# Output projection of feed-forward 1: gated tiles loaded through ScalarE's queue, ten weight tiles kept for the second pass, two rows of modulation computed in the mixer

## The chip, the core and the metric

The kernel runs on one core of a Trainium2 chip. The core has a matrix engine (TensorE, PE in the profile, with its weight loads as PEld), VectorE (DVE), ScalarE (ACT), GpSimd (POOL), SyncE (SP), which here only issues transfers, and 16 DMA engines that move data between device memory and the on-chip memory. Each engine executes its own instructions strictly in order. An instruction that waits holds back all that stand behind it on its engine; a transfer is started by an instruction too, here nearly always one of SyncE.

The metric is the time of one execution on the device in microseconds (us), median of three runs.

## The reference

One layer of a diffusion backbone works on 512 latent tokens and 256 context tokens of width 1024. Three sub-layers follow each other: a SwiGLU feed-forward of inner width 2816, a mixer (four heads of a chunkwise mLSTM and four groups of a pooling mixer), and a second feed-forward. Each is wrapped in RMS norms whose shift, scale and gate come from a modulation vector of nine rows of 1024 that is computed from the conditioning:

```
def ada_in(x, mod, j, g):
    return rmsnorm(x, g) * (1 + mod[:, 3 * j + 1, None]) + mod[:, 3 * j, None]

def ada_out(x, z, mod, j, g, res_w):
    return x + res_w * mod[:, 3 * j + 2, None] * rmsnorm(z, g)

def swiglu(y, w_in, w_out):
    a, b = jnp.split(y @ w_in, 2, axis=-1)
    return (jax.nn.silu(a) * b) @ w_out
...
        mod = (sc @ w_mod[l] + b_mod[l]).reshape(-1, N_MOD, D_MODEL)
        x = ada_out(x, swiglu(ada_in(x, mod, 0, norm_pre[l, 0]), ffn_w_in[l, 0], ffn_w_out[l, 0]),
                    mod, 0, norm_post[l, 0], 0.5)
        p = ada_in(x, mod, 1, norm_pre[l, 1]) @ w_in[l]
```

Rows 0 to 2 of the modulation belong to feed-forward 1, rows 3 to 5 to the mixer, rows 6 to 8 to feed-forward 2. The context tokens have a modulation of their own, which is needed up to row 4.

## The kernel before

All values are 32 bit. A product is formed as three matmuls of two halves: each operand is split into a high part (a rounding cast, ScalarE, line 81) and a low part (the difference, VectorE, line 78), and high times high, low times high and high times low are summed (`mm3`, lines 96 to 99, and `mm3p`, lines 107 to 110, through `mm` at line 102, whose order is fixed).

**Feed-forward 1** works on 768 tokens. For each of 22 inner tiles of 128 (f = 0 to 21) it computes the gated tile `silu(a) * b` (`in_fast`) and stores it to device memory (`g_d[f]`, line 492). The output projection then has two passes, `out_pass(0, ...)` and `out_pass(1, ...)`, each for 384 tokens (three token tiles) and all 22 inner tiles. They are called pass 1 and pass 2 in what follows. `prepare(f)` loads the tile of the output weight (line 756) and the gated tile (line 759) and splits both; `product` does the matmuls, 18 for each f, which accumulate in six banks of PSUM (`pa` and `pz`). The last two inner tiles of pass 1, and the last four of pass 2, are multiplied token tile by token tile, so that each token tile's sum is complete early. `done1`, through `ada_tile`, then normalises it: two squares of the sum (ScalarE, line 148), an inverse root on GpSimd (lines 159 and 143), gain and residual on VectorE (lines 175 and 179), the square of the result z (ScalarE, line 148 again), a second inverse root and the scaling (line 187). `back` transposes the result (TensorE, line 105), applies shift and scale (ScalarE, line 199) and splits it into `yh` and `yl` (lines 203 and 204), the operands of the mixer. `Backs` lets these transposes happen a number of steps (its lag) after their token tile. Pass 2 begins with the four inner tiles whose split weights are still in place, and then goes backward through the others. Latent token tiles also store z to device memory (`x1_d`, line 185).

**The modulation rows** 2 to 8 are computed beside this by `mod_steps`, a generator. A row (a block in the code) takes eight loads of a 128x1024 weight tile (line 676), each followed by one VectorE instruction for each stream that adds weight times conditioning to an accumulator (line 678; rows 2 to 4 have two streams, latent and context), and a last step: a sum over partitions on TensorE (line 688), the norm's gain (loaded in pieces, line 697; multiplied at line 698), and small stores of the row (line 704). `filler(n)` takes n steps; `mod_tick` takes one at most places of feed-forward 1, `out_pass` one or two after each inner tile. When row 4 is done, `begin_chain` loads and transposes what the passes' ends need.

**The mixer** begins with the value projection (lines 868 to 870 copy its results), whose gate columns go through a row of dependent instructions on VectorE and ScalarE (lines 880 to 935: logarithm of the forget gates, four scans along the tokens, exponentials). TensorE needs their results for transposes (`rows_to_columns`); until then it has projections as fillers. `MIX` lists the order of its steps by hand and how many microseconds of fillers stand between them.

Engines execute in the order that a scheduler has written: it may move an instruction ahead of others, except those that are pinned (`pin`, `keep_in_program_order`) relative to each other. Buffers come from pools: `m4` has 6 buffers, `raw` 5, `q3` 10.

## Time and profile before

| | |
|---|---|
| median of 3 runs | 1171.31 us (1171.27 to 1172.27) |
| the profiled execution | 1170.85 us, span of the trace 1169.1 us |
| granted TensorE clock, mean | 0.983 |
| TensorE busy | 1111.0 us (95% of the span) |
| VectorE busy | 894.8 us (77%) |
| ScalarE busy | 530.6 us (45%) |
| GpSimd busy | 106.4 us (9%) |
| DMA | 169.25 MB, mean 145 GB/s |
| feed-forward 1, inner products | to 372.4 us |
| output projection, pass 1 | 373.6 to 474.3 us |
| output projection, pass 2 | 485.6 to 590.1 us |

The span goes from the first to the last instruction; an execution has some 1.75 us around it. An engine's busy time doesn't say whether it bounds a stage: TensorE at 95% leaves 58 us in all, and where these lie is read from slices, from the timeline and from what ended each idle stretch.

### The profile page before, as it was taken

The numbers are of one execution on the slowest core, as the hardware profiler recorded it, in microseconds if no ns is written. First come the engines' busy times: TensorE is split into PE (matmuls) and PEld (weight loads), VectorE is DVE, ScalarE is ACT, GpSimd is POOL, SyncE is SP. The second block draws the span as 40 slices with busy tenths as digits, with TensorE's granted clock in tenths as the row PEclk, the third lists the DMA queues.
The fourth block names the chain that finished last, engine by engine and source line by source line (L and its number), as shares of the span: only waits on it lengthen the run. The fifth ranks groups of instructions, "written<-read, shape, count | busy, mean of one in ns | idle before, by whom it ended". The sixth has DMA issues, their size and how long they took to land.

```text
span 1169.1 us, 17262 instructions
## 1 busy us (share of the span) xinstructions
PE 1111.0 (95%) x6610; PEld 1004.8 (86%) x6610; DVE 894.8 (77%) x1315; ACT 530.6 (45%) x910; POOL 106.4 (9%) x139
## 2 busy tenths in 40 slices
PE   4999999999999999599899799999999999999996
PEld 3899999999998877478699687888999899999995
DVE  3798997898798676557445867875899898888865
ACT  4544333333333333464364556557665344444431
POOL 4000000000000000200122314412000000000001
PEclk9999999999999999799999899999999999999999
DMA  9933433643544887549623112134334333333321
GB/s 306 287 121 104 151 124 100 200 133 97 184 153 127 328 301 274 190 159 324 215 83 99 37 63 64 64 109 148 123 91 120 116 108 109 109 108 109 107 75 73
DMA packets 152673, 169.25 MB, mean 145 GB/s; under 512 B 7415, under 2 KB 125687, under 8 KB 152589
## 3 DMA queue, kind: packets, MB, share of 16 engines
q1 hardware_dynamic: 152540, 168.12, 44.6%
q8 instruction: 52, 0.85, 0.3%
q14 instruction: 33, 0.26, 0.1%
q10 hardware_dynamic: 48, 0.01, 0.0%
HBM read 153.12 MB, written 14.98 MB: 144 GB/s over the span
## 4 chain that ended last, share of the span: by engine, by line
PE 47%; DVE 6%; ACT 2%; DMA 1%; issue 1%; POOL 1%; SPq 0%; DVEq 0%; ACTq 0%; POOLq 0%
PE pa L102 9%; PE pa L98 7%; PE pa L99 7%; PE pa L97 7%; PE pz L102 4%; PE pz L97 3%; PE pz L98 3%; PE pz L99 3%; PE pt L102 3%; PE pt L105 1%; DVE wins L78 1%; DMA raw<-in_w_in_dram 1%; ACT junk L148 1%; DMA q<-g 0%; DVE z L179 0%
## 5 line engine op out<-in xcount | busy, mean ns | idle before, releaser
L97 PE MATMUL pa<-yh,wins 128*128 128x256 f32 (+1 forms) x768 | 236.2, 308 | 0.7 <-ACT yh L81 0.4
L99 PE MATMUL pa<-yl,wins 128*128 128x256 f32 (+1 forms) x768 | 235.9, 307 | 0.0
L98 PE MATMUL pa<-yh,wins 128*128 128x256 f32 (+1 forms) x768 | 235.8, 307 | 0.0
L78 DVE TENSOR_TENSOR wins<-raw,wins 128x1024 fp32r<-128x1024 f32 (+1 forms) x144 | 156.6, 1087 | 70.5 <-PE pa L98 39.8
L81 ACT CAST wins<-raw 128x1024 fp32r<-128x1024 f32 (+1 forms) x146 | 136.2, 935 | 110.5 <-PE pa L99 36.9
L97 PEld LDWEIGHTS pa<-yh,wins 128*128 128x128 f32 x768 | 145.0, 189 | 3.0 <-issue 0.8
L99 PEld LDWEIGHTS pa<-yl,wins 128*128 128x128 f32 x768 | 144.9, 189 | 0.5
L98 PEld LDWEIGHTS pa<-yh,wins 128*128 128x128 f32 x768 | 144.9, 189 | 0.5
L99 PE MATMUL pa<-tl,wins 128*128 128x384 f32 (+1 forms) x388 | 122.3, 315 | 0.0
L98 PE MATMUL pa<-th,wins 128*128 128x384 f32 (+1 forms) x388 | 121.8, 314 | 0.0
L97 PE MATMUL pa<-th,wins 128*128 128x384 f32 (+1 forms) x388 | 121.3, 313 | 0.0
L678 DVE SCALAR_TENSOR_TENSOR m<-m,sc,m 128x1024 f32<-128x1024 f32 x80 | 100.2, 1278 | 9.6 <-DMA m<-in_w_mod_dram 5.9
L81 ACT CAST wins<-sw 128x1024 fp32r<-128x1024 f32 x78 | 81.7, 1047 | 48.9 <-PE pa L99 35.5
L78 DVE TENSOR_TENSOR wins<-sw,wins 128x1024 fp32r<-128x1024 f32 x78 | 95.2, 1221 | 10.7 <-PE pa L98 7.0
L102 PE MATMUL pa<-yh,wins 128*128 128x512 f32 (+2 forms) x352 | 97.0, 362 | 0.0
L97 PEld LDWEIGHTS pa<-th,wins 128*128 128x128 f32 x388 | 72.8, 188 | 0.9 <-issue 0.8
L99 PEld LDWEIGHTS pa<-tl,wins 128*128 128x128 f32 x388 | 73.0, 188 | 0.1
L98 PEld LDWEIGHTS pa<-th,wins 128*128 128x128 f32 x388 | 73.0, 188 | 0.0
L102 PEld LDWEIGHTS pa<-yh,wins 128*128 128x128 f32 x352 | 62.0, 191 | 9.2 <-issue 2.2
L97 PE MATMUL pa<-wins,q 128*128 128x512 f32 x148 | 55.3, 407 | 8.9 <-ACT q L81 8.9
L102 PE MATMUL pa<-yl,wins 128*128 128x512 f32 (+2 forms) x176 | 62.4, 355 | 0.5 <-DVE yl L78 0.5
L98 PE MATMUL pa<-wins,q 128*128 128x512 f32 x148 | 59.3, 400 | 1.2 <-DVE q L78 1.2
(388 smaller groups left out, 2177.1 us busy)
## 6 DMA issues: line engine op xcount, KB each, us to landing
raw<-in_ffn_w_in_dram SPq DMA_DIRECT2D x87, 512.0 KB
raw<-in_ffn_w_out_dram SPq DMA_DIRECT2D x62, 512.0 KB
m<-in_w_mod_dram SPq DMA_DIRECT2D x57, 512.0 KB
g<-q SPq DMA_DIRECT2D x22, 384.0 KB
q<-g SPq DMA_DIRECT2D x44, 192.0 KB
raw<-in_w_in_dram SPq DMA_DIRECT2D x16, 512.0 KB
raw<-in_w_mod_dram SPq DMA_DIRECT2D x11, 512.0 KB
raw<-in_w_out_dram SPq DMA_DIRECT2D x16, 256.0 KB
```

The lines of the kernel that those rows point to most:

```text
L78: return eng.tensor_tensor(out=out_ap, in0=a, in1=b, op=ALU.subtract)
L81: return S.copy(hi, src)
L97: T.matmul(out_ap, lhsT=wh, rhs=xh, start=first, stop=False, **kw)
L98: T.matmul(out_ap, lhsT=wl, rhs=xh, start=False, stop=False, **kw)
L99: T.matmul(out_ap, lhsT=wh, rhs=xl, start=False, stop=last, **kw)
L102: return tc.keep_in_program_order(T.matmul(*args, **kw))
L105: return tc.keep_in_program_order(T.transpose(**kw))
L148: return S.activation(out=junk, in_=src, func=AF.Square, scale=D ** -0.5, accum_out=ssq)
L678: V.scalar_tensor_tensor(out=accs[st], in0=w, scalar=sc[:, st * KD + k:st * KD + k + 1], in1=accs[st], op0=ALU.mult, op1=ALU.add)
```

## The change

Five things are changed together. The gated tiles are loaded by ScalarE's queue instead of SyncE's, five inner tiles ahead (`fetch`, pinned), and so are the stores of z (`x1_d`), which moreover stand behind z's square now, and the small stores of the modulation rows. Ten weight tiles instead of four are kept split for pass 2; six of them lie in `yh` and `yl`, so the transposes that write these come 14 steps after their token tile instead of 4. Rows 7 and 8 of the modulation leave `out_pass`; they are computed in the mixer, a step at every fourth entry of `MIX` from the thirteenth on, with weights in `raw` and an accumulator of their own (`macc`). The norm's gain of a row is loaded ahead of its eight steps, where it isn't one of these two. `filler` is called at every tick of feed-forward 1 after the 17th, and in the passes once for every second inner tile.

```
@@ ada_tile
+        r2 = rstd1(z, junk)
         if store is not None:
-            load(store, z)
-        r2 = rstd1(z, junk)
+            put(store, z)
@@ done1
-                            lambda: q3()[:, 0:512], pin)
+                            lambda: q3()[:, 0:512], pin, nc.scalar.dma_start)
@@ mod_steps
-        def mod_steps():
-            for blk, streams in ((2, (0, 1)), (3, (0, 1)), (4, (0, 1)), (5, (0,)), (6, (0,)), (7, (0,)), (8, (0,))):
+        def mod_steps(blocks, new, acc, ahead):
+            for blk, streams in blocks:
...
+                res = gains() if ty and ahead else None
                 for k in range(KD):
-                    w = m4()
+                    w = new()
                     load(w, w_mod[k * P:(k + 1) * P, blk * D:(blk + 1) * D])
...
                 for st, i, g, cs in at:
-                    load(rows[(blk, st)][:, cs], res[g:g + 1])
+                    nc.scalar.dma_start(rows[(blk, st)][:, cs], res[g:g + 1])
                 yield blk
-        steps = mod_steps()
+        steps = mod_steps([(b, (0, 1)) for b in (2, 3, 4)] + [(b, (0,)) for b in (5, 6)], m4, m4, True)
@@ mod_tick
-            if next(count) % 4 < 3:
+            i = next(count)
+            if i % 4 < 3 or i > 16:
@@ out_pass
+            def fetch(f):
+                raws[f] = q3()[:, 0:384]
+                pin(nc.scalar.dma_start(raws[f], g_d[f][:, c0:c0 + 384]))
             def prepare(f):
...
-                r = q3()[:, 0:384]
-                load(r, g_d[f][:, c0:c0 + 384])
                 g = q3(F32R)
-                gs[f] = split_w(r, to=(g[:, 0:384], g[:, 384:NT]), keep=pin)
+                gs[f] = split_w(raws[f], to=(g[:, 0:384], g[:, 384:NT]), keep=pin)
...
+            for f in order[:5]:
+                fetch(f)
             for f in order[:2]:
                 prepare(f)
-            for f, later in zip(order[:-tail], order[2:]):
-                prepare(later)
+            for i, f in enumerate(order[:-tail]):
+                for g in order[i + 5:i + 6]:
+                    fetch(g)
+                prepare(order[i + 2])
...
-                filler(2 if half == 0 and f % 3 == 0 else 1)
+                if i % 2:
+                    filler(1)
@@ the passes
-        backs, first_backs = Backs(4), Backs(4)
+        backs, first_backs = Backs(4), Backs(14)
+        kept = order[-10:-4]
+        places = [y.rearrange("p k c -> p (k c)")[:, i * D:(i + 1) * D] for i in range(6) for y in (yh, yl)]
+        homes = {f: lambda i=i: (places[2 * i], places[2 * i + 1]) for i, f in enumerate(kept)}
...
-        for f in order[:-4]:
+        for f in order[:-10]:
             wos.pop(f)
-        order = order[-4:] + order[-5::-1]
+        order = order[-10:] + order[-11::-1]
@@ the mixer's loop
+        late = mod_steps([(7, (0,)), (8, (0,))], raw, lambda: pool.tile([P, D], F32, tag="macc", name="macc", bufs=1), False)
+        for i, step in enumerate(MIX.split()):
+            if i > 8 and i % 4 == 0:
+                next(late, None)
```

The scheduler's order moves at three places. The first is ScalarE at the border between the passes. Before, with the squares of the third token tile's sum (`pz`), the first transposes' results (L199, L203), the square of the third z (`thz`), and the first casts of pass 2:

```order
L148 ACTIVATE junk_116,sm_4307<-pz_3477 128x512
L148 ACTIVATE junk_116,sm_4307<-pz_3478 128x512
L199 ACTIVATE q3_4322<-pt_4323,ycol1_3623 128x128 x4
L203 CAST yh_103<-q3_4322 128x4x128
L148 ACTIVATE junk_116,sm_4344<-thz_3472 128x1024
L81 CAST q3_4360<-q3_4358 128x384
L81 CAST q3_4365<-q3_4363 128x384
```

The same place of the change:

```order
L148 ACTIVATE junk_116,sm_4247<-pz_3555 128x512
L148 ACTIVATE junk_116,sm_4247<-pz_3556 128x512
L148 ACTIVATE junk_116,sm_4271<-thz_3550 128x1024
L186 DMA x1_0_105<-thz_3550 128x1024
L763 DMA q3_4286<-g_12_129 128x384
L763 DMA q3_4288<-g_13_130 128x384
L763 DMA q3_4290<-g_14_131 128x384
L763 DMA q3_4292<-g_15_132 128x384
L763 DMA q3_4294<-g_16_133 128x384
L81 CAST q3_4296<-q3_4286 128x384
L81 CAST q3_4299<-q3_4288 128x384
```

The transposes' results are gone from here; a store and five loads stand between the last square and the first cast.

The second place is ScalarE at the start of pass 1, behind the last two activations of feed-forward 1 (L382, L385). Before:

```order
L382 ACTIVATE q3_3363<-pa_3367 128x384
L385 ACTIVATE q3_3363<-q3_3363 128x384
L81 CAST sw_3481<-raw_3479 128x1024
L81 CAST q3_3487<-q3_3485 128x384
L81 CAST wins_3492<-raw_3490 128x1024
```

The same place of the change:

```order
L382 ACTIVATE q3_3431<-pa_3435 128x384
L385 ACTIVATE q3_3431<-q3_3431 128x384
L763 DMA q3_3557<-g_0_117 128x384
L763 DMA q3_3559<-g_1_118 128x384
L763 DMA q3_3561<-g_2_119 128x384
L763 DMA q3_3563<-g_3_120 128x384
L763 DMA q3_3565<-g_4_121 128x384
L81 CAST sw_3569<-raw_3567 128x1024
L81 CAST q3_3573<-q3_3557 128x384
```

Five loads stand ahead of the first cast of pass 1. On VectorE two modulation steps (line 692 of the change) stand among the last four instructions of feed-forward 1, and four of row 6 stand directly ahead of the split of weight tile 18; all eight weight tiles of row 6 share one buffer of `m4`.

The third place is VectorE at the head of the mixer, from the copy of the forget gates (L881 before, L901 of the change) to the scans. Before:

```order
L881 COPY h4_5601<-h4_5600 64x768
L885 SCALAR_TENSOR_TENSOR h4_5602<-h4_5601 64x768
L893 MEMSET h4_5603 64x768
L896 MEMSET h4_5605 64x768
L894 MEMSET h4_5603 32x6
L895 MEMSET h4_5603 32x6
L888 SCALAR_TENSOR_TENSOR h4_5601<-h4_5601,h4_5602 64x768
L78 TENSOR_TENSOR wins_6031<-raw_6028,wins_6030 128x1024
L898 SCALAR_TENSOR_TENSOR h4_5604<-h4_5603,h4_5601 32x768
```

The same place of the change:

```order
L692 SCALAR_TENSOR_TENSOR macc_5855<-raw_5944,sc_99,macc_5855 128x1024
L901 COPY h4_5462<-h4_5461 64x768
L692 SCALAR_TENSOR_TENSOR macc_5855<-raw_5991,sc_99,macc_5855 128x1024
L905 SCALAR_TENSOR_TENSOR h4_5463<-h4_5462 64x768
L913 MEMSET h4_5464 64x768
L916 MEMSET h4_5466 64x768
L914 MEMSET h4_5464 32x6
L915 MEMSET h4_5464 32x6
L692 SCALAR_TENSOR_TENSOR macc_5855<-raw_6095,sc_99,macc_5855 128x1024
L692 SCALAR_TENSOR_TENSOR macc_5855<-raw_6133,sc_99,macc_5855 128x1024
L908 SCALAR_TENSOR_TENSOR h4_5462<-h4_5462,h4_5463 64x768
L78 TENSOR_TENSOR wins_5898<-raw_5895,wins_5897 128x1024
```

Four steps of row 7 stand in between here (L692). A fifth stands behind the second scan, and a sixth ahead of the first L1095 (L1075 before), which comes ahead of the copies of `tcol` (L959 before, L979 of the change).

## Rows read from the trace of the kernel before

**Rows 1.** Page, part 2: TensorE's busy tenths in 40 slices of 29.2 us.

```profile
PE   4999999999999999599899799999999999999996
```

**Rows 2.** Chain of waits, 355 to 700 us: start, us, what.

```profile
484.48 3.17 DMA q<-g
584.79 5.48 PE pz L102 x24
```

**Rows 3.** Timeline of TensorE, 455 to 500 us: start, us, instruction, count [idle before].

```profile
461.31 0.85 PE L102 MATMUL pa<-wins,q 128*128 128x512 f32 x3
465.18 6.30 PE L102 MATMUL pa<-wins,q 128*128 128x512 f32 x20 [0.81 <-DVE q L78]
471.31 2.94 PE L102 MATMUL pz<-wins,q 128*128 128x512 f32 x12
485.64 1.65 PE L97 MATMUL pa<-wins,q 128*128 128x512 f32 x3 [8.90 <-ACT q L81]
492.35 0.40 PE L97 MATMUL pz<-wins,q 128*128 128x512 f32 x1
```

**Rows 4.** Timelines of ScalarE and SyncE, 455 to 500 us.

```profile
484.04 1.06 ACT L148 ACTIVATE junk<-thz 128x1024 bf16<-128x1024 f32 x1 [0.90 <-DVE thz L179]
485.10 0.50 ACT L81 CAST q<-q 128x384 fp32r<-128x384 f32 x1
484.03 0.34 SPq L185 DMA_DIRECT2D x<-thz  x1
```

**Rows 5.** Windows: span, busy us of each engine, granted clock, DMA share, GB/s.

```profile
core 0: us, PE busy (x) PEld busy (x) DVE busy (x) ACT busy (x) POOL busy (x), PEclk, DMA share, GB/s
477.00:493.00 16.00, 6.16 (x15) 4.43 (x16) 10.64 (x15) 7.01 (x16) 3.87 (x7) 0.57 0.52 173
625.00:661.80 36.80, 28.66 (x166) 24.51 (x165) 32.56 (x51) 19.57 (x27) 15.31 (x11) 0.92 0.36 94
```

**Rows 6.** Timeline of TensorE, 555 to 600 us.

```profile
568.01 0.84 PE L102 MATMUL pa<-sw,q 128*128 128x512 f32 x3
573.03 0.49 PE L102 MATMUL pa<-wins,q 128*128 128x512 f32 x1 [2.83 <-ACT q L81]
590.11 0.60 PE L105 MATMUL pt<-ident,m 128*128 128x128 f32 x4
```

**Rows 7.** Timelines of ScalarE and SyncE, 540 to 600 us.

```profile
563.74 0.51 ACT L81 CAST q<-q 128x384 fp32r<-128x384 f32 x1 [9.25 <-DMA q<-g]
560.24 1.12 SPq L704 DMA_DIRECT2D row<-m  x4
561.41 0.34 SPq L759 DMA_DIRECT2D q<-g  x1
```

**Rows 8.** Timelines of VectorE and TensorE at the head of the mixer.

```profile
635.28 0.95 DVE L888 SCALAR_TENSOR_TENSOR h<-h,h 64x768 f32<-64x768 f32 x1 [1.43 <-ACT h L887]
658.29 2.08 DVE L1075 SCALAR_TENSOR_TENSOR h<-h,pcol,h 128x770 f32<-128x770 f32 x2 [0.53 <-ACT h L1072]
655.48 1.08 PE L105 MATMUL pt<-ident,h 128*128 128x128 f32 x6 [3.64 <-ACT h L927]
660.69 0.66 PE L105 MATMUL pt<-ident,h 64*128 64x64 f32 x4 [4.14 <-DVE tcol L959]
```

**Rows 9.** Instructions of line 678: min/median/max ns, first and last start.

```profile
L678 DVE SCALAR_TENSOR_TENSOR m<-m,sc,m x80: 1272/1278/1285, 112.8 to 541.6; 128x1024 f32<-128x1024 f32 x80
```

**Rows 10.** Timelines of TensorE, ScalarE and VectorE at pass 1's start.

```profile
372.39 1.06 PE L688 MATMUL pt<-m,ones 128*32 128x512 f32 x8
375.77 0.50 PE L98 MATMUL pa<-sw,q 128*128 128x512 f32 x1 [0.56 <-DVE q L78]
369.97 0.53 ACT L385 ACTIVATE q<-q 128x384 f32<-128x384 f32 x1 [3.31 <-DVE q L384]
372.49 0.56 DVE L392 TENSOR_TENSOR q<-q,pa 128x384 f32<-128x384 f32 x1 [0.89 <-PE pa L99]
374.03 1.22 DVE L78 TENSOR_TENSOR sw<-raw,sw 128x1024 fp32r<-128x1024 f32 x1
```

More of the change, by code (lines that the diff above doesn't have):

```diff
@@ L167, in tile_layer, with ada_tile @@
     x2_d = [dpool.tile([P, D], F32, name=f"x2_{t}") for t in range(4)]
-    def ada_tile(t, zs, z, halves, xr, gc, store, nxt, junk, half, keep=lambda ins: ins):
+    def ada_tile(t, zs, z, halves, xr, gc, store, nxt, junk, half, keep=lambda ins: ins, put=load):
         r = rstd2(halves)
@@ L664, in query_key, with gains @@
             S.mul(wqk, kc(p), float(P) ** -0.5)
-        def mod_steps():
-            for blk, streams in ((2, (0, 1)), (3, (0, 1)), (4, (0, 1)), (5, (0,)), (6, (0,)), (7, (0,)), (8, (0,))):
+        def mod_steps(blocks, new, acc, ahead):
+            for blk, streams in blocks:
                 accs = {}
+                j, ty = divmod(blk, 3)
+                nq = 4 // len(streams)
+                n = D // nq
+                at = [(st, i, 32 * (nq * st + i), slice(i * n, (i + 1) * n)) for st in streams for i in range(nq)]
+                def gains():
+                    gb = new()[:, 0:n]
+                    src = norm_pre if ty == 1 else norm_post
+                    for st, i, g, cs in at:
+                        load(gb[g:g + 32], src[j:j + 1, cs].broadcast_to([32, n]))
+                    return gb
                 for st in streams:
-                    accs[st] = m4()
+                    accs[st] = acc()
                     G.memset(accs[st], 0.0)
                     load(accs[st][0:1, :], b_mod[blk:blk + 1, :])
+                res = gains() if ty and ahead else None
                 for k in range(KD):
-                    w = m4()
+                    w = new()
                     load(w, w_mod[k * P:(k + 1) * P, blk * D:(blk + 1) * D])
@@ L681, in mod_steps @@
                 yield
-                nq = 4 // len(streams)
-                n = D // nq
-                at = [(st, i, 32 * (nq * st + i), slice(i * n, (i + 1) * n)) for st in streams for i in range(nq)]
                 p = pt()[:, 0:n]
@@ L688, in mod_steps @@
                     T.matmul(p[g:g + 32], lhsT=ones.broadcast_to([P, 32]), rhs=accs[st][:, cs], start=True, stop=True)
-                j, ty = divmod(blk, 3)
-                res = m4()[:, 0:n]
                 if ty == 0:
+                    res = new()[:, 0:n]
                     S.copy(res, p)
                 else:
-                    gb = m4()[:, 0:n]
-                    src = norm_pre if ty == 1 else norm_post
-                    for st, i, g, cs in at:
-                        load(gb[g:g + 32], src[j:j + 1, cs].broadcast_to([32, n]))
-                    V.scalar_tensor_tensor(out=res, in0=p, in1=gb, op1=ALU.mult,
+                    res = res if ahead else gains()
+                    V.scalar_tensor_tensor(out=res, in0=p, in1=res, op1=ALU.mult,
                                            **(dict(scalar=1.0, op0=ALU.add) if ty == 1 else
@@ L1255, in tile_layer @@
         queue = [sources[x[0]](*map(int, x[1:])) for x in QUEUE.split()]
-        for step in MIX.split():
+        late = mod_steps([(7, (0,)), (8, (0,))], raw, lambda: pool.tile([P, D], F32, tag="macc", name="macc", bufs=1), False)
+        for i, step in enumerate(MIX.split()):
+            if i > 8 and i % 4 == 0:
+                next(late, None)
             what, arg = step[0], step[1:]
@@ L1275, in tile_layer @@
                     {"w": hd.weights, "s": hd.states, "d": hd.decays, "o": hd.outputs}[what](int(arg[1]))
+        for _ in late:
+            pass
         junk = pool.tile([P, D], BF16, tag="un", name="junk2", bufs=2)
```

9 lines of the change are left out of this document (5 added, 4 removed).

## Prediction

> **What bounds the kernel now.** I read the page's slices first [rows 1]: TensorE is busy in nearly every slice, so the time can change only where its digit drops: slice 17 (467 to 497 us), slices 20 and 23, and what a change adds where it is full. Those places are the border between the two passes of the output projection, the end of the second pass, and the head of the mixer. The timeline of TensorE and what ended each idle stretch give each place; the chain of waits gives the price of a load and of a matmul at full speed: 24 matmuls in 5.48 us, 0.228 us each [rows 2].
>
> - End of pass 1: the last two tiles' 36 matmuls begin at 461.31 and end at 471.31 + 2.94 = 474.25 [rows 3]. At full speed they need 8.2 us, so 12.94 − 8.2 = 4.7 us is lost, of which 0.2 is the last matmul's tail: 4.5 us. They waited for the last tiles' splits.
> - Border: the second pass begins at 485.64, 11.4 us after the end; ScalarE casts its first gated tile only after the last token tile's square (484.04), which stands ahead of it on the same engine [rows 3, 4]. The load had landed. The next 12 matmuls take until 492.35, 6.71 us for 2.74 us of work: in this stretch the granted clock is 0.57, close to the lower level of 1.2 GHz, after TensorE stood idle [rows 3, 5].
> - End of pass 2: 72 matmuls from 568.01 to 590.11, 22.1 us for 16.4 [rows 6]: 5.7 us lost. ScalarE stood 9.25 us for a gated tile whose load SyncE issued only at 561.41, behind four small stores of a modulation row at 560.24 [rows 7].
> - Mixer: between 625 and 661.8 TensorE is busy 28.66 of 36.8 us, VectorE 32.56 [rows 5]; TensorE waits 3.64 us for ScalarE's L927 and 4.14 us for VectorE's L959 [rows 8], both ends of VectorE's row of scans.
>
> **The change, part by part.** I sum against the profiled execution, 1170.85 us (span 1169.1 and 1.75 around it); the median of the runs is 1171.31, 0.46 above, and the forecast is given on that.
>
> *End of pass 1: −4.5.* Of the 26 modulation loads in this pass 16 are left, and gated tiles are loaded five ahead, so the splits of tiles 18 to 21 should be done early. One thing is behind them: block 6 now has a single buffer for its weights, and four of its steps stand on VectorE directly ahead of tile 18's split. A step costs 1.28 us [rows 9] and its load about 3.2 [rows 2], so these four are a chain of some 18 us. Splits need only some 3 us a tile against 4.1 us (18 × 0.228) of matmuls, so by then they should be about four tiles (16 us) ahead, and two more tiles of matmuls lie between. I take the whole 4.5; the other end is 0.
>
> *Border: +2.6.* Before, the first gated tile lay ready. Now ScalarE's order is: third square, store of x1, five loads, then the cast. The three token tiles' chain stays as it was (square ends near 474.25 + 10.8; I give it 0.5 back, since VectorE's modulation steps beside it are gone), so 10.3. From a store's issue (484.03) to the landing of the gated tile issued behind it (484.48 + 3.17 = 487.65) took 3.6 us [rows 2, 4]; a cast takes 0.5 [rows 4]. TensorE starts at 10.3 + 3.6 + 0.5 = 14.4 us after the end instead of 11.4. Counting what is not work: before 11.4 − 0.45 (four transposes) + 3.97 (6.71 − 2.74) = 14.9; after 14.4 + about 3.1 (the same 6.4 us at half clock, without the wait for a low half in it) = 17.5. Ends: 0, if the loads are issued while ScalarE waits, which its order excludes, and +5. The kept weights save the loads and splits of six tiles here, but nothing waits for those loads.
>
> The Trainium skill ("DMA: Bandwidth & Descriptors", "Rules for kernel authors") advises to issue a transfer early and wait late, so that its fixed cost overlaps. Here it is issued late by its place on ScalarE; by that rule, with the load out before the squares, the border would cost 3.6 less. The trace agrees: before, the tile that was loaded early was cast without a wait for it, at 485.10.
>
> *Start of pass 1: +2.7.* The same on a smaller scale. ScalarE's last activation of feed-forward 1 ends at 369.97 + 0.53 = 370.5 [rows 10]; behind it now stand five loads. The first lands at 370.5 + 3.2, its cast ends at 374.2; TensorE, which did 1.16 us of row sums until 373.55 here and does these earlier now, is free at 372.39 [rows 10]. VectorE has two modulation steps among its last four instructions: the first takes the idle 0.89 before L392 and 0.4 more, the second 1.28, so the low half of the first weight tile moves from 374.03 to 375.6 and L98 from 375.77 to 377.3 [rows 10]. Loss then: 377.3 − 372.39 − 1.37 (six matmuls) = 3.5; before: 375.77 − 373.55 − 1.37 = 0.85. The difference is 2.7; ends 0 and 6.
>
> *End of pass 2: −5.7.* The gated tiles no longer stand behind SyncE's row stores, and ScalarE's order now has tiles 3 to 0 ahead of the casts of the mixer's value weights. Block 6's copy and four row stores stand ahead of tile 3 on ScalarE and wait for TensorE, but two tiles of matmuls (8.2 us) cover them, the copy and five issues of 0.34 [rows 7]; without this cover they would cost about 3. Ends −5.7 and 0.
>
> *Transposes* of the first half move from early to late in pass 2: same count, same cost. The six kept tiles' two splits each (1.2 us a tile on VectorE) were not waited for.
>
> *Head of the mixer: +7.4.* Block 7's steps are on VectorE in the row of scans. Two stand around L901, which waits for nothing else: +2.56 [rows 9]. Two stand between L905 and L908, where VectorE idled 1.43 us before [rows 8]: 2.56 − 1.43 = +1.1. One stands behind the first two scans: +1.28. That is +5.0 at TensorE's first wait (3.64). At the second (4.14), the copies that free its bank stood behind two L1075 of 1.04 us [rows 8]; now three or four and one more step stand ahead, of which 0.53 idle covers part: +2.4. Low end 0 (all hidden), high end 8 × 1.28 = 10.2. I take 7.4, since each inserted step stands between instructions that depend on each other.
>
> *Rest of the mixer: +1.5.* Eight steps of block 8, two times four row stores on ScalarE and two row sums. TensorE is full there and its fillers cover VectorE; ends 0 and 10.2, nearer to 0. The row sums that leave the passes (8 matmuls twice) come back here: 0.
>
> Sum: −4.5 + 2.6 + 2.7 − 5.7 + 7.4 + 1.5 = +4.0: 1174.85 by the profile, **1175.3** by the median. About 0.2% (2.3 us) is what a measurement tells from no change.
>
> **The rivals.**
> *Faster: the mixer hides block 7.* If VectorE's scans are not what TensorE waits for at 655 and 661, or the steps fall into its idle time, the 7.4 is gone: 1167.9. It decides from below 1.1 us in that place. For it: VectorE has 4.2 us idle between 625 and 661.8. Against it: only 2 of these lie where the steps are. Chance 0.2.
> *Half of it: no change.* Only the three steps that nothing can hide cost (3.8), and the rest falls together with ScalarE's table loads: 1171.7. Chance 0.12.
> *Slower: tile 18 late.* The single buffer's chain of 18 us is longer than the lead, TensorE waits for tile 18 and the 4.5 isn't won, or more is lost: 1180 to 1183. For it: splits were hardly a tile ahead before. Against it: ten of the 26 modulation loads that shared the pass with them are gone. Chance 0.15.
> *The gated loads were short of bandwidth, not of a queue.* Then ScalarE's queue brings nothing and the 5.7 stays: 1181. The trace: once issued, the load of 561.41 was there at 563.74, 2.3 us later [rows 7]. Chance 0.05. The Trainium skill speaks for this ("DMA: Bandwidth & Descriptors", "Issuing engines are not separate DMA queues"): transfers from any engine share the same 16 DMA engines, and another issuer saves only issuing time. The trace shows the issue itself held back by what is ahead on SyncE, which that rule leaves open.
>
> **How the numbers follow.** Forecast 0.48, rivals 0.2, 0.12, 0.15, 0.05. The forecast's own range is 1171 to 1180. With the rivals on both sides the range is 1166 to 1182. Faster 0.2; same 0.12 and 0.06 of the forecast's low side, 0.18; slower 0.62.
>
> **What would show it.** End of pass 1: no idle in the 36 matmuls. Border: TensorE idle 14 us, ScalarE's first cast waiting for the gated load, not for an engine. Start: L98 waiting some 2 us for VectorE. End of pass 2: 72 matmuls in 16.5 us. Mixer: the first wait of TensorE near 8.6 us, the second near 6.5, VectorE full from 630 on. The forecast is wrong if the mixer's waits stay near 3.6 and 4.1, if the border stays at 11, or if TensorE waits for tile 18.

## The result, and the profile after

The changed kernel takes 1189.87 us (median of 4 runs, 1188.3 to 1193.28) against 1171.3 us: ratio 1.016, interval 1.0136 to 1.0184, so 18.6 us slower. The forecast was 1175.3, slower, with a range up to 1182; the sign was right and the size was not. The profiled execution took 1188.92 us (span 1186.8). Of its page, the span, TensorE's slices (of 29.7 us each) and the granted clock, which answer to [rows 1]:

```profile
span 1186.8 us, 17172 instructions
...
PE   4999999999998999699997798899999999999996
...
PEclk9999999999999999799999799999999999999999
```

Counted from 1, slice 17 (475 to 504 us) is still the border. Slice 13 (356 to 386 us), where the first pass starts, has lost a tenth. In the mixer slices 22, 23, 25 and 26 stand below 9, where there was one. The timeline of TensorE of the changed kernel gives the places, in the columns of [rows 3]:

```profile
376.60 1.19 PE L97 MATMUL pa<-sw,q 128*128 128x512 f32 x4 [0.27 <-ACT q L81]
...
380.88 0.50 PE L98 MATMUL pa<-sw,q 128*128 128x512 f32 x1 [2.63 <-DVE q L78]
...
464.77 5.66 PE L102 MATMUL pa<-wins,q 128*128 128x512 f32 x24
470.27 2.90 PE L102 MATMUL pz<-wins,q 128*128 128x512 f32 x12
...
486.32 0.80 PE L97 MATMUL pa<-yh,q 128*128 128x512 f32 x1 [13.16 <-ACT q L81]
...
566.65 0.84 PE L102 MATMUL pa<-sw,q 128*128 128x512 f32 x3
...
583.08 0.60 PE L105 MATMUL pt<-ident,m 128*128 128x128 f32 x4
...
654.75 1.54 PE L105 MATMUL pt<-ident,h 128*128 128x128 f32 x6 [9.90 <-ACT h L947]
661.44 0.66 PE L105 MATMUL pt<-ident,h 64*128 64x64 f32 x4 [5.15 <-DVE tcol L979]
...
737.02 0.98 PE L698 MATMUL pt<-macc,ones 128*32 128x256 f32 x8 [2.37 <-issue]
...
761.62 1.51 PE L105 MATMUL pt<-ident,h 128*128 128x128 f32 x6 [2.67 <-DVE h L1215]
```

The 36 matmuls of the first pass's tail run through (464.77 to 473.17; before, waits of 1.69 and 0.81 us stood in them), and so do the 72 of the second pass's tail (566.65 to 583.08). The border waits 13.16 us. The second pass ends at 583.08, where it ended at 590.11 [rows 6]: the passes are 7.0 us ahead. In the mixer the first wait is 9.90 us instead of 3.64 and the second 5.15 instead of 4.14 [rows 8]. Then there are places that the prediction did not name: a row sum (L698) that waits 2.37 us at 737.02, and 2.67 us for VectorE's L1215 at 761.62.

VectorE's timeline shows the steps of rows 7 and 8 (L692, line 678 of before) where the order had them:

```profile
623.45 1.28 DVE L692 SCALAR_TENSOR_TENSOR macc<-raw,sc,macc 128x1024 f32<-128x1024 f32 x1
624.76 0.56 DVE L901 COPY h<-h 64x768 f32<-64x768 f32 x1
625.36 1.28 DVE L692 SCALAR_TENSOR_TENSOR macc<-raw,sc,macc 128x1024 f32<-128x1024 f32 x1
...
631.03 2.61 DVE L692 SCALAR_TENSOR_TENSOR macc<-raw,sc,macc 128x1024 f32<-128x1024 f32 x2 [1.80 <-DMA raw<-in_w_mod_dram]
...
744.66 1.28 DVE L692 SCALAR_TENSOR_TENSOR macc<-raw,sc,macc 128x1024 f32<-128x1024 f32 x1
745.85 0.68 DVE L1186 TENSOR_TENSOR h<-h,h 128x512 f32<-128x512 f32 x1
746.46 0.68 DVE L1187 TENSOR_TENSOR h<-h,h 128x512 f32<-128x512 f32 x1
...
747.83 1.28 DVE L692 SCALAR_TENSOR_TENSOR macc<-raw,sc,macc 128x1024 f32<-128x1024 f32 x1
...
749.42 1.28 DVE L692 SCALAR_TENSOR_TENSOR macc<-raw,sc,macc 128x1024 f32<-128x1024 f32 x1
```

At 631.03 two of them stand in front of a dependent instruction of the gate's row, and the first waits 1.80 us for its weight. Row 8's eight steps all lie between 744.66 and 766.8, among the score and output instructions of the heads (L1186, L1187 and their like). TensorE's window there (columns as in [rows 5]):

```profile
735.00:750.00 15.00, 12.98 (x69) 10.49 (x70) 11.79 (x26) 3.78 (x10) 3.85 (x4) 0.89 0.22 72
750.00:765.00 15.00, 11.30 (x49) 8.40 (x48) 13.34 (x29) 8.81 (x24) 2.08 (x4) 0.89 0.75 247
```

It is busy 12.98 and 11.30 of 15 us; the mean granted clock is 0.89 in both stretches, between the two levels of 1.2 and 2.4 GHz, and each has an idle stretch of over 2 us in it.

Since each execution starts the mixer at a slightly different time, the runs are compared by the time between the same instructions of TensorE in each trace: from the second pass's end (583.08 above) to the transposes after the second wait (**head**, 661.44), to the transposes for the third head's queries (**C**, 720.11), to the transposes of the second head's output (**D**, 738.53), of the third's (**E**, 766.42), of the fourth's (**F**, 792.28), and to the first transposes of the mixer's end (**G**, 814.83). The differences of their starts, in us:

| | head | C | D | E | F | G | mixer |
|---|---|---|---|---|---|---|---|
| before | 70.58 | 57.42 | 14.61 | 21.88 | 23.03 | 19.85 | 207.37 |
| the change | 78.36 | 58.67 | 18.42 | 27.89 | 25.86 | 22.55 | 231.75 |
| rows in the passes | 70.63 | 56.76 | 14.62 | 21.89 | 23.05 | 19.85 | 206.80 |
| row stores by SyncE | 78.64 | 58.45 | 18.52 | 29.24 | 24.97 | 22.63 | 232.45 |
| short steps | 74.85 | 57.97 | 18.43 | 22.30 | 25.03 | 22.44 | 221.02 |
| no row sum | 78.49 | 64.95 | 14.37 | 22.72 | 23.06 | 19.85 | 223.44 |
| denser steps | 76.82 | 62.09 | 24.85 | 21.42 | 23.05 | 19.85 | 228.08 |
| short steps and loads | 73.06 | 57.34 | 17.82 | 21.94 | 24.64 | 21.92 | 216.72 |
| short steps, no row sum | 74.84 | 58.72 | 18.33 | 20.91 | 23.04 | 19.85 | 215.69 |
| gated tiles by SyncE | 78.62 | 58.68 | 18.37 | 27.91 | 25.84 | 22.36 | 231.78 |
| rows alone | 78.33 | 56.47 | 15.47 | 33.27 | 29.25 | 28.47 | 241.26 |
| rows alone, one buffer | 78.71 | 57.85 | 17.80 | 29.27 | 24.75 | 22.53 | 230.91 |
| early border | 78.31 | 58.34 | 18.52 | 26.35 | 28.32 | 22.11 | 231.95 |
| put together | 70.62 | 57.18 | 14.61 | 21.87 | 23.05 | 19.85 | 207.18 |

The mixer lost 24.4 us: 7.8 in the head, where 7.4 were forecast, and 16.6 behind it (C 1.3, D 3.8, E 6.0, F 2.8, G 2.7), where 1.5 were forecast. With the 7.0 won before and 0.3 lost behind, that is the 17.7 us of the span. The rows below the second are the experiments.

What sets D is read from VectorE and GpSimd. A head's output is normalised by VectorE (L1227) before TensorE transposes it, with an inverse root from GpSimd (L143). In the changed kernel, VectorE and then GpSimd:

```profile
734.54 1.74 DVE L1227 TENSOR_TENSOR h<-h,sm 128x512 f32<-128x512 f32 x1 [2.44 <-POOL sm L143]
736.20 1.56 DVE L1169 SCALAR_TENSOR_TENSOR st<-st,cs_b,pt 128x129 f32<-128x129 f32 x4
...
732.23 1.29 POOL L1021 TENSOR_TENSOR h<-h 128x512 f32<-128x512 f32 x1
733.47 1.03 POOL L143 TENSOR_TENSOR sm<-sm,mhalf 128x4 f32<-128x4 f32 x1
```

And GpSimd in the kernel before:

```profile
728.90 1.03 POOL L143 TENSOR_TENSOR sm<-sm,mhalf 128x4 f32<-128x4 f32 x1
```

Counted from the end of C (720.11, before 718.11), L143 starts at 13.36 us instead of 10.79: GpSimd's order has four instructions of the pooling mixer (L1021) between there and L143, and had one before. L1227 starts at 14.43 instead of 11.86 us (L1207 before). The row sum at 737.02 stands behind the same wait. It takes one of the two banks of `pt`; the four instructions of L1169, which read `pt`, stand behind L1227, and it starts 0.1 us after the second of them. D is as before only in the runs where L143 stands in its early place: it starts at 10.55 to 10.80 us there and D is 14.37 to 14.62 (before, rows in the passes, no row sum, put together). Where it starts at 13.3 to 13.4 us, D is 17.8 to 18.5 (the change and six other runs); with the rows alone the two are 12.49 and 15.47, with short steps and no row sum 16.43 and 18.33, with denser steps 20.43 and 24.85. No run changed GpSimd's order alone.

### The profile page after: what moved, and what is told of

Its sections match the earlier page's. It is cut to its first block, busy times and chain, and to the rows that moved or that the text cites. A ratio compares the mean times of both kernels' runs of the same rounds, so it can differ in the third digit from the quotient of the medians.

```text
span 1186.8 us, 17172 instructions
## 1 busy us (share of the span) xinstructions
PE 1114.2 (94%) x6610; PEld 1007.3 (85%) x6610; DVE 887.6 (75%) x1309; ACT 523.9 (44%) x904; POOL 106.9 (9%) x139
## 3 DMA queue, kind: packets, MB, share of 16 engines
q10 hardware_dynamic: 7016, 10.80, 2.8%
## 4 chain that ended last, share of the span: by engine, by line
PE 46%; DVE 7%; ACT 2%; issue 2%; DMA 2%; POOL 1%; DVEq 0%; ACTq 0%; POOLq 0%
PE pa L102 8%; PE pa L97 7%; PE pa L98 7%; PE pa L99 7%; PE pz L102 4%; PE pz L97 3%; PE pz L98 3%; PE pz L99 3%; PE pt L102 2%; DVE wins L78 1%; PE pt L105 1%; ACT junk L148 1%; DVE h L1095 1%; DMA raw<-in_w_mod_dram 1%; DVE macc L692 0%
## 5 line engine op out<-in xcount | busy, mean ns | idle before, releaser
L98 PE MATMUL pa<-yh,wins 128*128 128x256 f32 (+1 forms) x768 | 236.0, 307 | 0.0
L78 DVE TENSOR_TENSOR wins<-raw,wins 128x1024 fp32r<-128x1024 f32 (+1 forms) x132 | 142.6, 1080 | 60.6 <-PE pa L98 30.1
L81 ACT CAST wins<-raw 128x1024 fp32r<-128x1024 f32 (+1 forms) x134 | 123.4, 925 | 122.7 <-PE pa L99 35.6
L98 PEld LDWEIGHTS pa<-yh,wins 128*128 128x128 f32 x768 | 144.9, 189 | 0.5
L98 PE MATMUL pa<-th,wins 128*128 128x384 f32 (+1 forms) x388 | 121.7, 314 | 0.0
L692 DVE SCALAR_TENSOR_TENSOR m<-m,sc,m 128x1024 f32<-128x1024 f32 x64 | 79.9, 1280 | 23.3 <-DMA m<-in_w_mod_dram 23.3
L98 PEld LDWEIGHTS pa<-th,wins 128*128 128x128 f32 x388 | 73.0, 188 | 0.0
L427 DVE TENSOR_TENSOR z<-z,pz 128x512 f32<-128x512 f32 x68 | 46.1, 685 | 17.4 <-PE pz L99 15.0
L97 PE MATMUL pz<-wos,gh 128*128 128x512 f32 x144 | 56.6, 393 | 1.8 <-DVE z L427 1.3
```

The costliest lines, as they stand in the source:

```text
L78: return eng.tensor_tensor(out=out_ap, in0=a, in1=b, op=ALU.subtract)
L81: return S.copy(hi, src)
L97: T.matmul(out_ap, lhsT=wh, rhs=xh, start=first, stop=False, **kw)
L98: T.matmul(out_ap, lhsT=wl, rhs=xh, start=False, stop=False, **kw)
L427: add = V.tensor_add(z[:, i, cols], z[:, i, cols], q)
L692: V.scalar_tensor_tensor(out=accs[st], in0=w, scalar=sc[:, st * KD + k:st * KD + k + 1], in1=accs[st], op0=ALU.mult, op1=ALU.add)
```

## The experiments

**Rows in the passes.** All of the change, but rows 7 and 8 stay where they were.

```
-        steps = mod_steps([(b, (0, 1)) for b in (2, 3, 4)] + [(b, (0,)) for b in (5, 6)], m4, m4, True)
+        steps = mod_steps([(b, (0, 1)) for b in (2, 3, 4)] + [(b, (0,)) for b in (5, 6, 7, 8)], m4, m4, True)
...
-                if i % 2:
-                    filler(1)
+                filler(2 if half == 0 and f % 6 == 0 else 1)
...
-            if i > 8 and i % 4 == 0:
-                next(late, None)
```

> The changed kernel with rows 7 and 8 of the modulation computed in feed-forward 1 and its passes again (one step per inner tile, two at every sixth tile of the first pass), everything else of the change kept. In the trace of the changed kernel the second pass ends 7.0 us earlier than before (583.08 against 590.11) and the mixer's end is 17.35 us later, so the mixer lost 24.4 us. Theory that all of the loss comes with the two rows in the mixer and that the passes' gain is the queue's and the kept weights': 1189.9 - 24.4 = 1165.5, up to 1168 with what 16 more loads and steps cost the passes. Rival that the gain of the passes came only from the rows having left them: 1171 or more, and the mixer's waits back at 3.6 and 4.1 us in both cases.

1172.37 us, ratio 1.0006 (0.9994 to 1.0019): no change. The mixer is as before, stretch for stretch, so all of its 24.4 us come with the two rows. But the passes' 7 us are gone too: the rival of this run was right. Both tails run without a wait, and the border waits 16.55 us, and 2.32 more at the first low half. The profiled execution (1177.09 us, 4.7 above the median) ends the second pass at 596.2. ScalarE's timeline shows a new wait in its first pass:

```profile
417.12 1.15 ACTq L710 DMA_DIRECT2D row<-m  x4
418.36 0.35 ACTq L763 DMA_DIRECT2D q<-g  x1
418.75 1.05 ACT L81 CAST wins<-raw 128x1024 fp32r<-128x1024 f32 x1 [15.27 <-DMA row<-m]
```

It stood 15.27 us, since the four row stores (L710) are on its queue, ahead of the next casts, and wait for the row's product with its gain on VectorE (L704, 416.67), which stands behind steps that waited 2.51 and 4.28 us for their weights; TensorE then waited 2.29 us at 423.05. The row stores had only moved from SyncE's queue [rows 7] to one that holds the splits.

**Row stores by SyncE.**

```
-                    nc.scalar.dma_start(rows[(blk, st)][:, cs], res[g:g + 1])
+                    (load if blk > 6 else nc.scalar.dma_start)(rows[(blk, st)][:, cs], res[g:g + 1])
```

> The changed kernel with the eight small stores of rows 7 and 8 issued by SyncE instead of ScalarE; TensorE's order is the same instruction for instruction. Theory A (the sixteen steps' time on VectorE costs the mixer): within 1 us of 1189.9. Theory B (the rows' ends cost it: ScalarE stands 8.7 us at 730 to 739 behind four stores that wait for the row sum): 3 to 6 us faster, and the 8.71 us of ScalarE gone. Theory C (weights share five buffers, so the mixer's and the next weights land late): within 1 us.

1190.61 us, ratio 1.0171 (1.0153 to 1.0188): no difference to the change. In the changed kernel ScalarE's timeline had shown the largest idle time behind the head at this place:

```profile
738.50 1.20 ACTq L710 DMA_DIRECT2D row<-raw  x4
739.75 0.37 ACT L1184 ACTIVATE h<-pz,cs_b 128x128 f32<-128x128 f32 x1 [8.71 <-DMA row<-raw]
```

With the stores gone from ScalarE, the same place:

```profile
740.29 0.37 ACT L1184 ACTIVATE h<-pz,cs_b 128x128 f32<-128x128 f32 x1 [8.19 <-DVE h L1182]
```

The stores were only the last of what ScalarE waited for: it still stands 8.19 us, now until VectorE's L1182, which stands behind VectorE's wait for GpSimd's L143 (2.44 us in this run too). So the stores' place costs nothing; what the idle time itself costs, this run does not show.

**Short steps.** The multiply-adds of rows 7 and 8 cover 32 columns.

```
-                        V.scalar_tensor_tensor(out=accs[st], in0=w, ...
+                        c = D if ahead else 32
+                        V.scalar_tensor_tensor(out=accs[st][:, 0:c], in0=w[:, 0:c], ...
```

> The changed kernel with the sixteen multiply-adds of rows 7 and 8 cut to 32 of their 1024 columns (the rest of those rows stays the bias), all loads, row sums and stores kept. It takes some 16 x 1.2 = 19 us off VectorE in the mixer. Theory A: 15 to 20 us faster (1170 to 1175), the waits at the head back near 3.6 and 4.1 us. Theory B or C: only the head's 7.7 us come back, and 8 or more of the 16.6 us between 661 us and the mixer's end stay: 1177 to 1183.

1177.68 us, ratio 1.0057 (1.0042 to 1.0072): 12 us faster than the change. The time lies at the lower edge of what theories B and C gave (1177 to 1183), and 9.4 of the 16.6 us behind the head stay, as they said; but the head has given back only 3.5 of its 7.8 us, which no theory had. In the table E is back (22.30), D, F and G are not. VectorE's timeline says what holds the rest of the head:

```profile
624.66 0.25 DVE L693 SCALAR_TENSOR_TENSOR macc<-raw,sc,macc 128x32 f32<-128x32 f32 x1 [0.88 <-DMA raw<-in_w_mod_dram]
...
630.90 0.78 DVE L693 SCALAR_TENSOR_TENSOR macc<-raw,sc,macc 128x32 f32<-128x32 f32 x1 [1.01 <-DMA raw<-in_w_mod_dram]
...
656.84 0.25 DVE L693 SCALAR_TENSOR_TENSOR macc<-raw,sc,macc 128x32 f32<-128x32 f32 x1 [2.13 <-DMA raw<-in_w_mod_dram]
```

Three waits, 4.0 us together, for row 7's weights: a short step too holds up what stands behind it until its load has landed.

**No row sum.** The sum over partitions of rows 7 and 8 is left out.

```
-                p = pt()[:, 0:n]
-                for st, i, g, cs in at:
+                p = pt()[:, 0:n] if ahead else accs[0][:, 0:n]
+                for st, i, g, cs in at if ahead else ():
```

> The changed kernel without the sum over partitions of rows 7 and 8 (the row is taken from one partition's part), so no matmul of TensorE and no PSUM bank stands between the steps and the stores; steps, loads and stores kept. Theory A or C: 2 to 4 us faster (sixteen short matmuls, 2.4 us of wait). Theory B: 6 to 10 us faster, since TensorE no longer waits for a bank at 737 us, its clock stays up, and ScalarE's stores no longer wait for it.

1181.06 us, ratio 1.0094 (1.0075 to 1.0112): 8.8 us faster than the change. D and G are back at 14.37 and 19.85: 4.1 and 2.7 us. Without the sum the single accumulator was free sooner, row 8's steps moved to 690 to 731 us, E and F are back (8.0 us together), and C is 6.3 us longer than in the change. VectorE's timeline has a wait for row 8's weights in it:

```profile
695.28 1.28 DVE L692 SCALAR_TENSOR_TENSOR macc<-raw,sc,macc 128x1024 f32<-128x1024 f32 x1 [3.37 <-DMA raw<-in_w_mod_dram]
```

So the steps were dear there too, but this run doesn't say how much of the 6.3 us they cost and how much the wait. Nor does it show that the sum cost D its 4.1 us: GpSimd's L143 is back at its early place in this run as well.

**Denser steps**, at every second entry of the list (`i % 2 == 0`), so that row 8 starts earlier with its row sums kept.

> The changed kernel with a late step at every second entry of the mixer's list instead of every fourth, so that row 7's sum stands earlier on TensorE and row 8, which has the same single accumulator, starts earlier. Theory B (the row sum at 737 us holds the only accumulator, so row 8's eight steps crowd VectorE from 744 to 766): the steps of row 8 spread from about 700 us and 5 to 8 us come back, 1182 to 1185. Theory A (10 us more of VectorE's work cost the same wherever they stand): within 2 us of 1189.9. The head's 7.8 us stay in both.

1188.21 us, ratio 1.0125 (1.0103 to 1.0147): some 2 us, the mixer 3.7 by its profile. Row 8 moved to 715 to 740 us, E, F and G are back, and C and D are 9.8 us longer. Row 8's first step waits there, for the bias that is loaded into its accumulator:

```profile
715.39 1.28 DVE L692 SCALAR_TENSOR_TENSOR macc<-raw,sc,macc 128x1024 f32<-128x1024 f32 x1 [6.84 <-DMA macc<-in_b_mod_dram]
```

The load was issued at 713.84, once GpSimd had cleared the accumulator (712.85, L685), behind 9 us of the pooling mixer's instructions. So spreading the steps brought no net gain, but it is not shown that crowding is free: a wait took its place.

**Short steps and loads**: in the run with short steps, the loads of those weights are cut to 32 columns too.

> The run with short steps once more (the multiply-adds of rows 7 and 8 cut to 32 columns), with their sixteen weight loads cut to 32 columns too. With short steps alone the head of the mixer still took 4.3 us more than before (74.85 us from the second pass's end to the transposes after the second wait, against 70.58), with VectorE waiting 0.88, 1.01 and 2.13 us for those weights. Theory that these weights land late, because they share five buffers with the mixer's own: the head is back at 70.6 to 71.5 us, 1173 to 1174. Rival that the place of the steps in VectorE's order costs it: the head stays at 74.9, 1177.7.

1175.14 us, ratio 1.0033 (1.002 to 1.0046). The head is at 73.06: 1.8 of the remaining 4.3 us came back, and one wait of 2.53 us for such a load was left. So the late weights are a part of it, as much as their size sets; the rest, how long a load stands behind others for its buffer, this run doesn't separate.

**Short steps and no row sum** together.

> Short steps and no row sum together in the changed kernel (rows 7 and 8 hold partial values), all loads kept. Behind the head the mixer lost 16.6 us; short steps gave 7.2 of them back, the run without row sums 8.4. Theory that they are two separate costs: 15 of the 16.6 come back, 138 us from the second wait to the mixer's end against 136.8 before, 1169 to 1171. Rival that one covers the other: 1175 or more.

1177.52 us, ratio 1.0054 (1.0035 to 1.0073), with runs from 1173.26 to 1181.77; by its profile the mixer takes 215.69 us, 16.1 less than in the change. That execution is the fastest of the six, 4.3 us below their median; by the medians the run gains nothing on short steps alone, which is what the rival said. Behind the head 12.5 of 16.6 us came back, not 15. In C VectorE waits for weights (3.18 and 2.46 us the longest), and D stays at 18.33 though its row sum is gone: VectorE waits there for GpSimd.

```profile
734.95 0.69 DVE L1228 TENSOR_TENSOR h<-h,sm 128x512 f32<-128x512 f32 x1 [4.64 <-POOL sm L143]
```

The two costs add up only in part; late weights and GpSimd's order fill in.

**Rows alone.** The kernel before with rows 7 and 8 in the mixer, and nothing else of the change.

```
+        late = mod_steps([(7, (0,)), (8, (0,))], raw, lambda: pool.tile([P, D], F32, tag="macc", ...
+        for i, step in enumerate(MIX.split()):
+            if i > 8 and i % 4 == 0:
+                next(late, None)
```

> The kernel before with one part of the change alone: rows 7 and 8 of the modulation are computed in the mixer, as in the changed kernel; gated tiles, stores, four kept weight tiles and one or two steps per inner tile as before. From the first runs the rows in the mixer cost 24.4 us there (206.8 us from the second pass's end to the mixer's end with the rows in the passes, 231.75 with them in the mixer). Theory that the passes gain only from the rows having left them: they gain some 7 us here too, 1171 + 24.4 - 7 = 1188. Theory that the queue and the kept weights bring the 7 us: 1195.

1196.17 us, ratio 1.0201 (1.0183 to 1.0218). The second pass ends at 579.2, 10.9 us sooner than before, with SyncE's queue and four kept tiles; its tail has no wait. The mixer costs 33.9 us more than before. SyncE's timeline at D:

```profile
704.71 0.39 SPq L114 DMA_DIRECT2D raw<-in_w_in_dram  x1
730.33 1.12 SPq L704 DMA_DIRECT2D row<-raw  x4
...
735.09 0.80 SPq L1226 DMA_DIRECT2D raw<-in_w_out_dram  x2
```

Between 704.71 and 730.33 it issued nothing; the next weights of the mixer's output projection came at 735.09, behind the row's end, and E, F and G are 3 to 6 us longer than in the change. Here a row's end takes two of the five buffers that it shares with the mixer's weights (one for the gain, one for its product). So:

**Rows alone, one buffer**: the product is written over the gain's tile, as in the change.

```
-                res = new()[:, 0:n]
...
+                    res = gb if blk > 6 else new()[:, 0:n]
```

> The kernel before with rows 7 and 8 in the mixer, as in the earlier run of that part alone, but with the product of row sum and gain written over the gain's tile, as in the change, so that a row's end takes one of the five weight buffers instead of two. That run's mixer took 241.3 us against 231.75 in the changed kernel. Theory that the second buffer held back the mixer's output weights: the mixer is at 232 us, 1187. Rival that the row stores on SyncE held them back: 1196.

1185.41 us, ratio 1.0111 (1.0093 to 1.0129); the mixer is at 230.91 us. One buffer was worth 10 us. The passes end at 582.37, as in the change. The whole loss is there with the rows alone: this run is 4.5 us below the change, with intervals that do not meet, so the queue, the kept tiles and the loads ahead brought nothing beside the rows.

**Gated tiles by SyncE** in the changed kernel.

```
-                pin(nc.scalar.dma_start(raws[f], g_d[f][:, c0:c0 + 384]))
+                load(raws[f], g_d[f][:, c0:c0 + 384])
```

> The changed kernel with the gated tiles' loads on SyncE's queue again (still five ahead in the code), all else of the change kept, rows 7 and 8 in the mixer. Theory that their place on ScalarE costs the starts of both passes, and that the tail of the second pass no longer needs them there once the stores of rows 7 and 8 are gone: border and start each 2 to 4 us shorter, 1183 to 1187. Rival that SyncE's queue holds them behind weight loads, so that a tail waits again: 1190 or more.

1187.54 us, ratio 1.0126 (1.0108 to 1.0144), an interval that overlaps that of the change. TensorE's timeline, the border and the second pass's end:

```profile
484.31 0.80 PE L97 MATMUL pa<-yh,q 128*128 128x512 f32 x1 [10.51 <-ACT q L81]
486.11 0.79 PE L98 MATMUL pa<-yh,q 128*128 128x512 f32 x1 [1.01 <-DVE q L78]
...
582.57 0.60 PE L105 MATMUL pt<-ident,m 128*128 128x128 f32 x4
```

The border waits 10.51 us instead of 13.16, as expected, but the start of the first pass still waits 2.71 us at L98, and the pass ends at 582.57, within 0.5 us of the change, without a wait in its tail. ScalarE's queue won nothing here; the trace of before had the load behind row stores [rows 7], and in this run no row store is left on SyncE. The Trainium skill ("DMA: Bandwidth & Descriptors", "Issuing engines are not separate DMA queues") says that another issuer saves only the time of issuing; this run agrees, by its 0.5 us.

**Border opened early**, in the changed kernel: fetches go on into the second pass, four of its tiles are split ahead of the first pass's last products, and its first four inner tiles run token tile by token tile.

```
+                (job if job.queue else following or job).fetch()
...
+                for f in following.order[:ready]:
+                    following.prepare(f)
...
+            for j in range(3):
+                for f in order[:head]:
+                    for h in range(2):
+                        product(f, j, h, mm3)
```

> The changed kernel with the second pass opened early: its first five gated tiles are loaded as the first pass's run out, its first four are split ahead of the first pass's last products, and its first four inner tiles are multiplied token tile by token tile, so that each needs only its own banks. Theory that the border's 13.2 us of wait and 3 us at the lower clock come from the loads and casts standing behind the last square on ScalarE: TensorE does not wait at the border, 12 to 16 us faster, 1174 to 1178. Rival, that the banks of the first pass (freed by the gain's multiplication on VectorE, 5.5 us for each token tile) hold the start: 5 us faster, with waits for VectorE at the border instead.

1173.33 us, ratio 1.0003 (0.9987 to 1.0018): 16.5 us below the change. TensorE's timeline at the border:

```profile
472.20 2.90 PE L102 MATMUL pz<-wins,q 128*128 128x512 f32 x12
474.93 0.39 PE L97 MATMUL pa<-yh,q 128*128 128x512 f32 x1
```

It goes from the last product of the first pass (the 12 matmuls of 472.20) into the second at 474.93 without a wait. The rival fell, that the banks hold it: each token tile's sum is read while the others are multiplied, and no wait for it shows. The mixer is as dear as in the change (231.95 us).

**Put together**, a version that beats both: rows 7 and 8 in the passes, the border opened early, and

```
-                    nc.scalar.dma_start(rows[(blk, st)][:, cs], res[g:g + 1])
+                    nc.gpsimd.dma_start(rows[(blk, st)][:, cs], res[g:g + 1])
...
-                    gb = new()[:, 0:n]
+                    gb = pool.tile([P, 512], F32, tag='gn', name='gn', bufs=1)[:, 0:n]
...
-            if i % 4 < 3 or i > 16:
+            if i < 34 and (i % 4 < 3 or i > 16):
...
+                filler((i % 2 if i < 18 else 0) if half == 0 else 3 if i < 7 else 2 if i < 14 else 1)
```

> Put together from the first runs: rows 7 and 8 back in the passes (most steps in the second pass, whose first ten weight tiles are not loaded), the second pass opened early as in the run before this, the small row stores issued by GpSimd instead of ScalarE, which stood 15 us behind them in the run with the rows in the passes, the gains in a buffer of their own, and no step at the last two places of feed-forward 1. From 1172.4 with the rows in the passes: border -15, start of the first pass -2.5: 1155. If the border's waits only move to VectorE: 1166. If the steps of the second pass hold its splits: 1172 or more.

1159.08 us, ratio 0.9886 (0.9869 to 0.9903): 13 us faster than before. Its page:

```profile
span 1157.0 us, 17248 instructions
...
PE   4999999999999899989999799999999999999996
...
PEclk9999999999999999999999899999999999999999
```

The border's slice is at 9 now. The start of the first pass, which should have won 2.5 us, did not (3.70 us of wait for VectorE there, 384.07), and the second pass has one wait of 3.24 us for VectorE at 506.35; the forecast was 1155.

## Why the prediction was wrong

**The step that failed is "Rest of the mixer: +1.5"**, which measured +16.6, beyond the 10.2 of its upper end. It was wrong in two of its statements. "TensorE is full there and its fillers cover VectorE": TensorE's busy share says that it has work, not that VectorE's work is off the path. The short steps gave back 7.2 us behind the head, 5.6 of them in E, where row 8's eight steps stood. That is 70% of their 10.2 us; the upper end was much nearer than the 1.5 taken. "The row sums that leave the passes come back here: 0": row 8's sum stands in G, and G is back at 19.85 in every run that has no sum there, 2.7 us shorter; F is back in the same runs, but what it waits for isn't shown.

Two further costs had no term. One is the order of a third engine. D is 3.8 us longer; 2.6 of them are there already when VectorE begins the output's norm, behind GpSimd's L143, and about 1 us is left for the row sum at 737.02. This is read from the traces and was not tried by itself. The other is the loads: the weights of the two rows share five buffers with the mixer's own, land late and hold what waits for them, and behind it all that follows on the same engine. In the changed kernel VectorE waits so once, 1.80 us in the head, and ScalarE's casts of the mixer's weights wait 1.24 and 1.86 us behind it (727.93 and 757.84); in the run with one buffer more taken the mixer lost 10 us more. How the 16.6 us divide is settled only within some us, since each cost fills in where another is taken away.

**Head of the mixer, +7.4: right in size (7.8), half right in cause.** The first wait grew by 6.3 us (5.0 forecast), the second by 1.0 (2.4). The steps' own time is 3.5 us of it, by the short steps; 4.3 remain with the steps short, and late weights are part of that. The sum had counted the steps in full and no load.

**The passes, -4.9 in all, measured -7.0; the cause was named wrongly.** Their places came out: no wait in either tail (-4.5 and -5.7 us, as forecast), 2.63 us at L98 in the start (+2.3 counted as the prediction does, +2.7 forecast), a border of 13.16 us (14 forecast) whose first cast waits for its load. ScalarE's timeline of the changed kernel shows that last step:

```profile
482.08 1.06 ACT L148 ACTIVATE junk<-thz 128x1024 bf16<-128x1024 f32 x1 [3.03 <-DVE thz L179]
482.13 0.35 ACTq L186 DMA_DIRECT2D x<-thz  x1
482.52 1.25 ACTq L763 DMA_DIRECT2D q<-g  x2
...
485.76 0.99 ACT L81 CAST q<-q 128x384 fp32r<-128x384 f32 x2 [2.53 <-DMA q<-g]
```

The store and the first loads are issued as the last square starts, not when it ends, and the cast waits 2.53 us. The border costs 0.8 us instead of 2.6: TensorE starts 13.15 us after the end of the first pass, not 14.4, and its first 12 matmuls take 5.30 us (486.32 to 491.62), where 6.71 had been. L98 itself comes 3.6 us later than forecast (380.88): the pass starts later, with the transposes and products of the query weights, which stood inside it (L658 and L662, 383 to 388 us), now made ahead of it (359 to 367 us). But the gain was put down to ScalarE's queue and to loading ahead, and the runs say that it comes from the rows that left: the rows alone moved the end of the second pass by -10.9 and -7.7 us, the change without them moved the time by nothing. The second tail's waits are gone in either case. Those of the first tail stay with the rows alone (1.77 us) and are gone in the change without them, which then pays at the border (16.55 us). So the forecast of the tails was right in size partly by luck: the second tail's gain did not hang on the queue that it was put down to.

**The rivals.** "The mixer hides block 7" and "half of it" fell with the head. "Tile 18 late" does not show in the changed kernel's profile; but the profiled executions of the runs without row sum and with denser steps have waits of 2.05 and 2.58, and of 0.58 and 2.54 us there (456 to 461 us), so it is near its edge. "Short of bandwidth" fell: in the changed kernel and with the gated tiles by SyncE no gated tile was waited for in the second pass's tail.

## What to carry to other kernels

Work that is moved into a stage is priced by the row of dependent instructions that it enters, not by the busy share of the engine that bounds the stage: here 16 short VectorE steps, two sums and 16 loads that were to fit beside a full TensorE cost 24 us. Count with a moved step its loads' buffers and its end (a sum on TensorE, a bank, stores) as well, and first move it in the kernel as it was, alone. The name that a trace gives a long idle time is only the last of what it waited for: with the stores gone, ScalarE's 8.71 us were 8.19 with another name. An instruction that is moved can also change the order of an engine that it does not use, as GpSimd's here; read that order too before the result is explained. Opening the next loop's operands ahead of the last one's end was worth more than any queue.

## What was not expected of the hardware

One instruction takes different times in the gate's row of VectorE: the first scan over 32x768 took 2.78 us in the kernel before (L898, 637.36, GpSimd busy from 636.75) and 1.74 us in the changed one (L918, 635.56, GpSimd busy only from 637.93). The next scan of the changed kernel (L920, 637.33) took 1.75 us with GpSimd at work for most of it, so overlap alone doesn't explain it. What the two traces do show is a difference at the start: the four scans of this size that began while a GpSimd instruction was running took 2.31 to 2.78 us (L898, L900 and L907 before, L927 in the changed kernel), the two that began with GpSimd idle took 1.74 and 1.75 us. No run was made on it.
